# Every second gate and up pair of three feed-forward blocks by seven block products in place of eight

## The chip, the cores and the metric

The kernel runs on one core of a Trainium2 chip. The metric is device microseconds of one execution; lower is better. The inputs are float32, and the result is compared with a float32 reference.

## The reference

512 tokens of width 1024 go through a first block (a mixer, then a squared-ReLU feed-forward of width 4096, then a norm) and through two layers of a second block. Each of these layers has a gated feed-forward, a mixer (attention with pooling in layer 0, a short convolution in layer 1) and a second gated feed-forward, each with a modulated norm ahead of it:

```python
def swiglu(h, wg, wu, wd):
    return (jax.nn.silu(h @ wg) * (h @ wu)) @ wd
...
    for l in range(DEPTH_2):
        mod = (c_act @ w_ada[l] + b_ada[l]).reshape(b, N_MOD, 1, D_MODEL)
        sh1, sc1, g1, sh2, sc2, g2, sh3, sc3, g3 = [mod[:, i] for i in range(N_MOD)]
        h = modulated_norm(x, norm_g[l, 0], sh1, sc1)
        x = x + 0.5 * g1 * swiglu(h, ffn_wg[l, 0], ffn_wu[l, 0], ffn_wd[l, 0])
        ...
        h = modulated_norm(x, norm_g[l, 2], sh3, sc3)
        x = x + 0.5 * g3 * swiglu(h, ffn_wg[l, 1], ffn_wu[l, 1], ffn_wd[l, 1])
```

`h` is 512 x 1024, `wg` and `wu` are 1024 x 2816, `wd` is 2816 x 1024.

## The kernel before

Activations lie transposed: a tile has 128 features as partitions and the 512 tokens as columns, so `h` is eight tiles. Each value is kept as two float32r parts, a rounded one and the remainder (`h[:, 0]`, `h[:, 1]`). A weight block is treated likewise: ACT casts it to `whi`, DVE subtracts to get `wlo`. One product is then three matmuls per 128 features: high by high, high by low, low by high (`mm3`, L146 to L148):

```python
        nc.tensor.matmul(o, lhsT=hi[:, k, :], rhs=x[:, 0, t0:t0 + tn], start=first, stop=False)
        nc.tensor.matmul(o, lhsT=hi[:, k, :], rhs=x[:, 1, t0:t0 + tn], start=False, stop=False)
        nc.tensor.matmul(o, lhsT=lo[:, k, :], rhs=x[:, 0, t0:t0 + tn], start=False, stop=last)
```

A gated block (`ffn_glu`, `ffn`) has 22 pairs: pair m holds 128 columns of the gate weights and 128 of the up weights, 1 MB in one load. `wload` (L123) brings it into one of two staging tiles; `wblock` casts (L135) and subtracts (L136) the two units into two of four `whi` and two of four `wlo` buffers; `gemm` makes 24 matmuls for the gate and 24 for the up product, each group into one of five PSUM banks (`acc`). `evac` applies Silu to the gate (ACT, L768), multiplies by the up product (DVE, L770), and `split` writes the two parts of `y` (ACT L211, DVE L212). After 8, 7 and 7 pairs, `down` multiplies the `y` so far by its part of `wd` and adds the result to the residual (L306). All y, h and some attention tiles share a pool of 20 slots (`act`).

The last `down` of a block is tied to the next norm: `sumsq` gathers squares, and `norm_parts` computes, for each half of the tokens, the scale (`sums`) and the tiles (`tiles`: L276 makes the scaled `ht` in one of two buffers, L283 adds the shift and rounds, L284 makes the low part). `lead` then runs the first two pairs of the next block on the first 256 tokens, while the second half of the norm is still being made, and after it on the second 256.

The modulation (`ada_setup`) is 72 steps, each a 1 MB load into one buffer and two multiply-and-sum instructions on DVE (L790). `wblock` starts one step each time it is called (`ada_step`), except in the attention, where they are held back. The first block's feed-forward, the first gated block and the stage after the attention carry them.

Nothing in the text fixes the order on an engine, except where it asks for it: the program is traced, and a scheduler issues each engine's instructions by priority (place in the text) and readiness in its own model of the chip. Between `order_pe` and `free_pe` PE keeps the order of the text; before the change that is from the last two products of a `down` with a norm to the end of `lead`. Each engine works through its instructions in the order written, and a load waits on SP's queue for its buffer.

Of the kernel before, what the change touches and what calls it, by code (L numbers as in the profile page):

```python
# [17 lines left out]
T = 512  # L18
# [8 lines left out]
class Net:  # L27
    def __init__(self, ctx, tc, a, out):
        self.ctx, self.tc, self.nc, self.a, self.out = ctx, tc, tc.nc, a, out
        pool = lambda name, bufs, **kw: ctx.enter_context(tc.tile_pool(name=name, bufs=bufs, **kw))  # L30
        self.const = pool("const", 1)
        self.act = pool("act", 20)
        self.xv = pool("xv", 4)
        self.stg = pool("stg", 2)
        self.whl = pool("whl", 4)
        self.work = pool("work", 2)
        self.acc_p = pool("acc", 5, space=PSUM)
        self.ms_p = pool("ms", 3, space=PSUM)
        self.ada_todo = []
        self.ada_hold = False  # L40
        self.tail, self.late = [], []
        self.setup()

# [210 lines left out]

    def norm_parts(self, hs, half, gcols, shcols, pre=None):
        nc = self.nc
# [13 lines left out]
        def tiles():  # L270
# [3 lines left out]
            for k in range(8):  # L274
                t = self.wk("ht", (128, 256), 2)
                nc.vector.scalar_tensor_tensor(out=t, in0=self.xs(k, t0, 256), scalar=gcols[:, k:k + 1],  # L276
# [20 lines left out]
    def down(self, src, kn, xs, gcol, nxt=None, opened=()):  # L297
# [48 lines left out]
        if pre is not None:  # L346
            g = self.wk("fg", (128, 8), 1)
            nc.vector.tensor_tensor(out=g, in0=nxt["g"], in1=pre, op=ALU.mult)
        parts = [self.norm_parts(hs, half, g, nxt.get("sh"), pre) for half in range(2)]
        self.order_pe()  # L350
# [22 lines left out]
    def lead(self, wus, hs, done):  # L373
        for c, (part, t0) in enumerate((((0, 1, 2), 0), ((3,), 0), ((0, 1), 256), ((2, 3), 256))):
# [6 lines left out]
            for ps, j in zip(pss, part):  # L381
                done(j, ps, t0)

    def mixer1(self):
# [321 lines left out]

    def ffn(self, hs, groups, upblk, evac, dnsrc, gcol, nxt):
        m0 = 0
        for gi, gn in enumerate(groups):
# [22 lines left out]
            while len(ys) < gn:  # L732
                ws, outs = upblk(m0 + len(ys))
                n = len(ws) // outs
                for o in range(outs):
                    d = self.slot("y")
                    pss = [self.gemm([w], hs)[0] for w in ws[n * o:n * o + n]]
                    evac(d, pss, 0, 512)
                    ys.append(d)
            last = gi == len(groups) - 1  # L740
            r = self.down(dnsrc(gi), gn, ys, gcol, nxt if last else None)
            m0 += gn
# [17 lines left out]
    def ffn_glu(self, hs, l, i, gcol, nxt):  # L760
# [11 lines left out]

        return self.ffn(hs, FF2_GROUPS, up, evac, lambda gi: a[f"w_dn_{l}{i}{gi}"], gcol, nxt)

    def ada_setup(self):
        nc, a = self.nc, self.a
        c = self.ada_p = self.ctx.enter_context(self.tc.tile_pool(name="ada", bufs=1))
        self.SS2 = c.tile([128, 512], F32, name="SS2")
        cb = c.tile([128, 1024], F32, name="cb")
        nc.gpsimd.dma_start(out=cb, in_=a["c_rep"])  # L780
        nc.scalar.activation(out=cb, in_=cb, func=AF.Silu)
        self.mod = [c.tile([128, 72], F32, name=f"mod{l}") for l in range(2)]
        self.dmod = [c.tile([128, 48], F32, name=f"dmod{l}") for l in range(2)]

# [24 lines left out]
    def nspec(self, l, n):  # L809
        return {"g": self.dmod[l][:, 16 * n:16 * n + 8], "sh": self.mod[l][:, 24 * n:24 * n + 8]}  # L810

    def gate(self, l, n):
# [313 lines left out]
    def run(self):  # L1126
# [5 lines left out]
        for l in range(2):  # L1132
            hs = self.ffn_glu(hs, l, 0, self.gate(l, 0), self.nspec(l, 1))
            hs = (self.attn if l == 0 else self.conv)(hs, self.nspec(l, 2), self.gate(l, 1))
            hs = self.ffn_glu(hs, l, 1, self.gate(l, 2), self.nspec(1, 0) if l == 0 else "out")

# [111 lines left out]
```

## Time and profile before

| | us |
|---|---|
| median of three runs (2736.5 to 2742.88) | 2737.88 |
| the profiled execution | 2739.53 |
| its span, first to last instruction | 2737.4 |
| PE busy in it | 2696.5 |
| DVE busy | 1425.5 |
| ACT busy | 856.5 |

The granted clock was 0.997 over the span. The page gives busy time by engine, the groups of instructions by line and the loads. Queries of the trace give waits by engine (who waited, for whom, how long), single instructions in order of time, and busy time in chosen stretches. A matmul's duration is modelled; the distance between the starts of neighbours is not.

### The profile page before, as it was taken

To read this page: it belongs to the slowest core of one execution; us is meant where nothing else is said; L and a number is where in the kernel's file an instruction comes from. 1 tells how busy PE (TensorE), PEld (TensorE's weight loads), DVE (VectorE), ACT (ScalarE), POOL (GpSimd) and SP (SyncE) were. 2 spreads that over 40 slices of the span, in tenths; PEclk is the share of its full clock that TensorE was granted. 3 is DMA by queue.
4 is the path that set the end of the run, shared out by engine and by line. 5 is a ranking of instruction groups with operands and counts; after the bars stand their busy time and mean duration, and the time that the engine had idled before them with its cause. 6 is when DMAs were issued, how large, how long until landed. Compare 5 with 4: busy or idle time off the path is not lost.

```text
span 2737.4 us, 32001 instructions
## 1 busy us (share of the span) xinstructions
PE 2696.5 (99%) x13188; PEld 2273.0 (83%) x13188; DVE 1425.5 (52%) x2282; ACT 856.5 (31%) x1288; POOL 69.0 (3%) x98
## 2 busy tenths in 40 slices
PE   8999999999999999999999999999999999999999
PEld 6888888788888888888878888888888888888888
DVE  6556733476656855557676333353333454533333
ACT  5322222333223322224553222232222332332221
POOL 0000000000000000001210000000000000000000
PEclk9999999999999999999999999999999999999999
DMA  4211133355455455553223232323222223233232
GB/s 170 75 65 51 40 129 104 125 189 185 185 202 197 147 197 210 197 180 134 80 104 127 93 102 91 102 76 108 93 99 96 97 81 104 79 106 101 91 106 72
DMA packets 51281, 327.96 MB, mean 120 GB/s; under 512 B 5776, under 2 KB 6416, under 8 KB 17088
## 3 DMA queue, kind: packets, MB, share of 16 engines
q1 hardware_dynamic: 50400, 323.37, 33.8%
q0 software_dynamic: 736, 2.56, 0.3%
q8 instruction: 103, 1.69, 0.2%
q14 instruction: 42, 0.34, 0.0%
HBM read 323.81 MB, written 2.10 MB: 119 GB/s over the span
## 4 chain that ended last, share of the span: by engine, by line
PE 90%; DVE 5%; DMA 2%; issue 1%; ACT 1%; POOL 1%; SPq 0%; DVEq 0%; POOLq 0%; ACTq 0%
PE acc L147 27%; PE acc L146 27%; PE acc L148 27%; PE ms L590 2%; DMA ada<-in_w_ada 1%; DVE wlo L136 1%; PE acc L179 1%; PE acc L180 1%; PE acc L178 1%; DVE ada L790 1%; PE ms L628 1%; PE acc L206 1%; PE acc L205 1%; PE acc L204 0%; PE ms L568 0%
## 5 line engine op out<-in xcount | busy, mean ns | idle before, releaser
L135 ACT CAST whi<-w 128x1024 fp32r<-128x1024 f32 (+1 forms) x468 | 482.1, 1030 | 1537.7 <-PE acc L147 1434.0
L146 PE MATMUL acc<-h,whi 128*128 128x512 f32 (+1 forms) x2352 | 891.6, 379 | 9.0 <-ACT h L283 5.4
L147 PE MATMUL acc<-h,whi 128*128 128x512 f32 (+1 forms) x2352 | 885.7, 377 | 8.6 <-DVE h L284 5.1
L148 PE MATMUL acc<-h,wlo 128*128 128x512 f32 (+1 forms) x2352 | 883.5, 376 | 0.0
L136 DVE TENSOR_TENSOR wlo<-w,whi 128x1024 fp32r<-128x1024 f32 (+1 forms) x468 | 559.9, 1197 | 460.4 <-ACT whi L135 449.0
L147 PEld LDWEIGHTS acc<-h,whi 128*128 128x128 f32 x2352 | 445.3, 189 | 89.1 <-DVE h L284 6.8
L146 PEld LDWEIGHTS acc<-h,whi 128*128 128x128 f32 x2352 | 445.1, 189 | 88.8 <-ACT h L283 6.6
L148 PEld LDWEIGHTS acc<-h,wlo 128*128 128x128 f32 x2352 | 445.1, 189 | 77.5
L146 PE MATMUL acc<-y,whi 128*128 128x512 f32 (+1 forms) x1112 | 415.5, 374 | 0.0
L147 PE MATMUL acc<-y,whi 128*128 128x512 f32 (+1 forms) x1112 | 414.6, 373 | 0.0
L148 PE MATMUL acc<-y,wlo 128*128 128x512 f32 (+1 forms) x1112 | 414.4, 373 | 0.0
L147 PEld LDWEIGHTS acc<-y,whi 128*128 128x128 f32 x1112 | 209.5, 188 | 37.6 <-DVE y L212 0.9
L146 PEld LDWEIGHTS acc<-y,whi 128*128 128x128 f32 x1112 | 209.6, 188 | 36.8
L148 PEld LDWEIGHTS acc<-y,wlo 128*128 128x128 f32 x1112 | 209.5, 188 | 36.3
L790 DVE SCALAR_TENSOR_TENSOR ada<-ada,cb 128x1024 f32<-128x1024 f32 x144 | 174.8, 1222 | 105.9 <-DMA ada<-in_w_ada 105.8
L306 DVE SCALAR_TENSOR_TENSOR xt<-acc,dmod,xt 128x512 f32<-128x512 f32 (+1 forms) x124 | 86.6, 698 | 250.9 <-PE acc L148 250.7
L770 DVE TENSOR_TENSOR e<-acc,e 128x512 f32<-128x512 f32 (+1 forms) x92 | 60.3, 656 | 228.1 <-PE acc L148 227.8
L211 ACT CAST y<-e 128x512 fp32r<-128x512 f32 (+1 forms) x140 | 81.5, 583 | 56.4 <-DVE e L755 37.1
L212 DVE TENSOR_TENSOR y<-e,y 128x512 fp32r<-128x512 f32 (+1 forms) x140 | 89.4, 640 | 9.0 <-ACT y L211 8.9
L590 PEld LDWEIGHTS ms<-kq 128*128 128x128 f32 x448 | 56.3, 192 | 3.1
L283 ACT ACTIVATE h<-ht,mod 128x256 fp32r<-128x256 f32 x96 | 44.0, 502 | 45.6 <-DVE ht L276 45.6
L304 DVE TENSOR_TENSOR xt<-xt,acc 128x512 f32<-128x512 f32 (+1 forms) x44 | 28.0, 637 | 55.6 <-PE acc L148 55.6
(268 smaller groups left out, 2089.4 us busy)
## 6 DMA issues: line engine op xcount, KB each, us to landing
w<-in_w_gu SPq DMA_DIRECT2D x88, 1024.0 KB, 4.9
ada<-in_w_ada SPq DMA_DIRECT2D x72, 1024.0 KB, 6.4
w<-in_w_ff SPq DMA_DIRECT2D x32, 1024.0 KB, 4.8
w<-in_w_dn SPq DMA_DIRECT2D x32, 896.0 KB, 4.5
w<-in_w_dn SPq DMA_DIRECT2D x16, 1024.0 KB, 4.8
w<-in_w_fq SPq DMA_DIRECT2D x8, 1024.0 KB, 4.8
w<-in_w_gg SPq DMA_DIRECT2D x8, 1024.0 KB, 6.1
w<-in_w_cx SPq DMA_DIRECT2D x8, 1024.0 KB, 4.8
```

The costliest lines, as they stand in the source:

```text
L135: nc.scalar.copy(hi[:, :n], w[:, o:o + n])
L136: nc.vector.tensor_tensor(out=lo[:, :n], in0=w[:, o:o + n], in1=hi[:, :n].bitcast(F32), op=ALU.subtract)
L146: nc.tensor.matmul(o, lhsT=hi[:, k, :], rhs=x[:, 0, t0:t0 + tn], start=first, stop=False)
L147: nc.tensor.matmul(o, lhsT=hi[:, k, :], rhs=x[:, 1, t0:t0 + tn], start=False, stop=False)
L148: nc.tensor.matmul(o, lhsT=lo[:, k, :], rhs=x[:, 0, t0:t0 + tn], start=False, stop=last)
L211: nc.scalar.copy(h, src)
L212: nc.vector.tensor_tensor(out=dst[:, 1, t0:t0 + tn], in0=src, in1=h.bitcast(F32), op=ALU.subtract)
L283: nc.scalar.activation(out=h, in_=t, func=AF.Identity, bias=shcols[:, k:k + 1])
L306: nc.vector.scalar_tensor_tensor(out=x, in0=ps[:, :tn], scalar=gcol[:, m:m + 1], in1=x, op0=ALU.mult, op1=ALU.add)
L590: nc.tensor.matmul(ps[:, c * 64:(c + 1) * 64].rearrange("p (n b) -> p n b", b=b), lhsT=K[:, s], rhs=half(Q[:, s], 1), start=True, stop=True)
L770: nc.vector.tensor_tensor(out=y, in0=pss[1][:, :tn], in1=t, op=ALU.mult)
L790: nc.vector.scalar_tensor_tensor(out=w[:, i, :], in0=w[:, i, :], scalar=1.0, in1=cb, op0=ALU.mult, op1=ALU.mult, accum_out=self.mod[l][:, ...
```

## The change

In the last three gated blocks (layer 0's second, layer 1's first and second) the pairs 3, 5, ... 21 are computed by a seven-product scheme for 2 x 2 blocks: the weights of a pair are cut into gate and up by two halves of the 1024 features, the tokens into two halves of 256. `seven` makes four sums of weight blocks (three in a tile `S`, one in place in the staging tile), seven casts, their low parts in four subtractions, seven products of four feature tiles and 256 tokens each, and puts gate and up together again in `U`. `token_sums` makes the four sums of token blocks once per block, after pair 2, from the scaled norm tiles, which are kept in four slots (`keep`) in place of the two `ht` buffers. PE's order is that of the text from pair 3 up to the block's last `down`. The modulation's results move to another pool, so that its pool can be closed after the attention and its space be used for the sums; `ffn` starts two more modulation steps ahead of each `down` of the squared-ReLU block.

```diff
-    def norm_parts(self, hs, half, gcols, shcols, pre=None):
+    def norm_parts(self, hs, half, gcols, shcols, pre=None, keep=None):
...
-                t = self.wk("ht", (128, 256), 2)
+                t = self.wk("ht", (128, 256), 2) if keep is None else keep[k // 2][:, k % 2, t0:t0 + 256]
...
+        keep = None
+        if "sums" in nxt:
+            keep = self.B = [self.act.tile([128, 2, 512], F32, tag="slot", name="hb") for _ in range(4)]
+            self.sh = nxt["sh"]
...
+    def hilo(self, dst, src):
+        nc = self.nc
+        nc.scalar.copy(dst[:, 0], src)
+        nc.vector.tensor_tensor(out=dst[:, 1], in0=src, in1=dst[:, 0].bitcast(F32), op=ALU.subtract)
+
+    def token_sums(self, hs):
+        nc = self.nc
+        B, sh = self.B, self.sh
+        self.B = None
+        pairs = lambda t: t.rearrange("p a (k n) -> p a k n", k=2)
+        ds = self.wk("dsh", (128, 4), 1)
+        nc.vector.tensor_tensor(out=ds, in0=sh[:, 4:8], in1=sh[:, 0:4], op=ALU.subtract)
+        T = [[], [], [], []]
+        for j in range(2):
+            b1, b2 = B[j], B[2 + j]
+            b11, b12, b21, b22 = b1[:, :, 0:256], b1[:, :, 256:512], b2[:, :, 0:256], b2[:, :, 256:512]
+            for i in range(4):
+                T[i].append(pairs(self.slot("T") if i == 2 else self.slot("T", self.sx)))
+            nc.vector.tensor_tensor(out=b11, in0=b12, in1=b11, op=ALU.subtract)
+            self.hilo(T[0][j], b11)
+            for i in range(2):
+                k = 2 * j + i
+                nc.vector.scalar_tensor_tensor(out=b12[:, i], in0=b22[:, i], scalar=ds[:, k:k + 1], in1=b12[:, i],
+                                               op0=ALU.add, op1=ALU.subtract)
+            self.hilo(T[2][j], b12)
+            for i in range(2):
+                nc.vector.scalar_tensor_tensor(out=b22[:, i], in0=b22[:, i], scalar=sh[:, 4 + 2 * j + i:5 + 2 * j + i],
+                                               in1=b11[:, i], op0=ALU.add, op1=ALU.subtract)
+            self.hilo(T[1][j], b22)
+            for i in range(2):
+                nc.vector.scalar_tensor_tensor(out=b21[:, i], in0=b21[:, i], scalar=sh[:, 4 + 2 * j + i:5 + 2 * j + i],
+                                               in1=b22[:, i], op0=ALU.add, op1=ALU.subtract)
+            self.hilo(T[3][j], b21)
+        tok = lambda t: [(t[k // 2][:, 0, k % 2], t[k // 2][:, 1, k % 2]) for k in range(4)]
+        blk = lambda k0, n0: [(hs[k0 + k][:, 0, n0:n0 + 256], hs[k0 + k][:, 1, n0:n0 + 256]) for k in range(4)]
+        self.rhs = {1: blk(0, 0), 2: blk(4, 0), 3: blk(4, 256), 4: tok(T[3]), 5: tok(T[0]), 6: tok(T[1]), 7: tok(T[2])}
+
+    def seven(self, src, d):
+        nc = self.nc
+        w = self.wload(src)
+        S = self.sx.tile([128, 1536], F32, tag="S", name="S", bufs=1)
+        A = [w[:, 512 * i:512 * i + 512] for i in range(4)]
+        S1, S2, S4 = (S[:, 512 * i:512 * i + 512] for i in range(3))
+        op = {}
+
+        def parts(src, ps):
+            n = 512 * len(ps)
+            hi = self.whl.tile([128, 1024], F32R, tag="whi", name="whi")
+            lo = self.whl.tile([128, 1024], F32R, tag="wlo", name="wlo")
+            for i, p in enumerate(ps):
+                c = slice(512 * i, 512 * i + 512)
+                nc.scalar.copy(hi[:, c], src[:, c])
+                op[p] = tuple(t[:, c].rearrange("p (k m) -> p k m", m=128) for t in (hi, lo))
+            nc.vector.tensor_tensor(out=lo[:, :n], in0=src, in1=hi[:, :n].bitcast(F32), op=ALU.subtract)
+
+        def comb(out, a, b, how):
+            nc.vector.tensor_tensor(out=out, in0=a, in1=b, op=how)
+
+        parts(w[:, 0:1024], (1, 2))
+        comb(S1, A[2], A[3], ALU.add)
+        comb(S2, S1, A[0], ALU.subtract)
+        parts(S[:, 0:1024], (5, 6))
+        comb(A[2], A[0], A[2], ALU.subtract)
+        comb(S4, A[1], S2, ALU.subtract)
+        parts(w[:, 1024:2048], (7, 4))
+        parts(S4, (3,))
+        self.ada_step()
+
+        def prod(p):
+            ps = self.acc()[:, 0:256]
+            hi, lo = op[p]
+            for k in range(4):
+                xh, xl = self.rhs[p][k]
+                nc.tensor.matmul(ps, lhsT=hi[:, k, :], rhs=xh, start=(k == 0), stop=False)
+                nc.tensor.matmul(ps, lhsT=hi[:, k, :], rhs=xl, start=False, stop=False)
+                nc.tensor.matmul(ps, lhsT=lo[:, k, :], rhs=xh, start=False, stop=(k == 3))
+            return ps
+
+        U = self.sx.tile([128, 4, 256], F32, tag="U", name="U", bufs=1)
+        p1, u2, u3, v = (U[:, i] for i in range(4))
+        e = self.wk("e1", bufs=3)
+        y = self.wk("e2")
+        nc.scalar.copy(p1, prod(1))
+        comb(u2, prod(6), p1, ALU.add)
+        comb(e[:, 0:256], prod(2), p1, ALU.add)
+        comb(u3, prod(7), u2, ALU.add)
+        ps = prod(5)
+        comb(u2, ps, u2, ALU.add)
+        comb(v, ps, u3, ALU.add)
+        comb(e[:, 256:512], prod(3), u2, ALU.add)
+        nc.scalar.activation(out=e, in_=e, func=AF.Silu)
+        comb(y[:, 256:512], v, e[:, 256:512], ALU.mult)
+        comb(v, prod(4), u3, ALU.add)
+        comb(y[:, 0:256], v, e[:, 0:256], ALU.mult)
+        self.split(d, y)
...
             while len(ys) < gn:
-                ws, outs = upblk(m0 + len(ys))
+                m = m0 + len(ys)
+                if seven is not None and m >= 3 and m % 2:
+                    if m == 3:
+                        self.order_pe()
+                    d = self.slot("y")
+                    self.seven(seven(m), d)
+                    ys.append(d)
+                    continue
+                ws, outs = upblk(m)
...
+                if seven is not None and m == 2:
+                    self.token_sums(hs)
             last = gi == len(groups) - 1
+            if last and seven is not None:
+                self.free_pe()
+            for _ in range(2 if gcol is None else 0):
+                self.ada_step()
             r = self.down(dnsrc(gi), gn, ys, gcol, nxt if last else None)
...
-        c = self.ada_p = self.ctx.enter_context(self.tc.tile_pool(name="ada", bufs=1))
+        self.ada_es = ExitStack()
+        c = self.ada_p = self.ada_es.enter_context(self.tc.tile_pool(name="ada", bufs=1))
...
-            hs = (self.attn if l == 0 else self.conv)(hs, self.nspec(l, 2), self.gate(l, 1))
-            hs = self.ffn_glu(hs, l, 1, self.gate(l, 2), self.nspec(1, 0) if l == 0 else "out")
+            if l:
+                xs.close()
+            hs = (self.attn if l == 0 else self.conv)(hs, self.sums_spec(l, 2), self.gate(l, 1))
+            if l == 0:
+                self.ada_es.close()
+                xs = ExitStack()
+                self.sx = xs.enter_context(self.tc.tile_pool(name="sums", bufs=6))
+            else:
+                self.sx = self.ctx.enter_context(self.tc.tile_pool(name="sums2", bufs=6))
+            hs = self.ffn_glu(hs, l, 1, self.gate(l, 2), self.sums_spec(1, 0) if l == 0 else "out")
```

## Rows read from the trace of the kernel before

**Rows 1.** Page, part 1: busy us (share of the span) xinstructions, by engine.
```profile
PE 2696.5 (99%) x13188; PEld 2273.0 (83%) x13188; DVE 1425.5 (52%) x2282; ACT 856.5 (31%) x1288; POOL 69.0 (3%) x98
```

**Rows 2.** Waits of PE, whole span: waiter, what released it, total, times, longest.
```profile
PE acc L146 <- ACT h L283: 5.4, 5, 2.0
PE acc L147 <- DVE h L284: 5.1, 6, 1.3
...
PE ms L105 <- DVE mod L802: 0.8, 1, 0.8
```

**Rows 3.** Timeline of PE: first and last of 110, then of 50 matmuls.
```profile
2382.92 0.28 PE L147 MATMUL acc<-h,whi 128*128 128x256 f32 x1
...
2396.00 0.28 PE L148 MATMUL acc<-h,wlo 128*128 128x256 f32 x1
...
2396.82 0.40 PE L146 MATMUL acc<-h,whi 128*128 128x512 f32 x1
...
2407.93 0.39 PE L147 MATMUL acc<-h,whi 128*128 128x512 f32 x1
```

**Rows 4.** Groups of DVE by form: busy us, mean ns | idle before, releaser.
```profile
L136 DVE TENSOR_TENSOR wlo<-w,whi 128x1024 fp32r<-128x1024 f32 x396 | 484.5, 1225 | 411.9 <-ACT whi L135 402.0 <-PE ms L431 3.0
...
L212 DVE TENSOR_TENSOR y<-e,y 128x512 fp32r<-128x512 f32 x116 | 79.5, 686 | 8.9 <-ACT y L211 8.9
...
L770 DVE TENSOR_TENSOR e<-acc,e 128x512 f32<-128x512 f32 x80 | 55.3, 691 | 228.0 <-PE acc L148 227.8 <-issue 0.2
L284 DVE SCALAR_TENSOR_TENSOR h<-ht,mod,h 128x256 fp32r<-128x256 f32 x96 | 42.8, 480 | 2.1 <-ACT h L283 1.9
...
L212 DVE TENSOR_TENSOR y<-e,y 128x256 fp32r<-128x256 f32 x24 | 9.9, 420 | 0.1
```

**Rows 5.** Groups of ACT by form, same columns.
```profile
L135 ACT CAST whi<-w 128x1024 fp32r<-128x1024 f32 x396 | 416.6, 1052 | 1296.4 <-PE acc L147 1192.8 <-issue 59.9 <-PE acc L180 29.4
L211 ACT CAST y<-e 128x512 fp32r<-128x512 f32 x116 | 72.0, 621 | 53.6 <-DVE e L755 36.9 <-DVE e L770 16.4
...
L768 ACT ACTIVATE e<-acc 128x512 f32<-128x512 f32 x80 | 47.0, 588 | 0.0
...
L768 ACT ACTIVATE e<-acc 128x256 f32<-128x256 f32 x16 | 6.1, 381 | 11.7 <-PE acc L148 11.7
```

**Rows 6.** Timeline of DVE: start, us, instruction, idle before it.
```profile
2402.68 1.23 DVE L136 TENSOR_TENSOR wlo<-w,whi 128x1024 fp32r<-128x1024 f32 x1 [2.69 <-ACT whi L135]
2407.30 0.69 DVE L770 TENSOR_TENSOR e<-acc,e 128x512 f32<-128x512 f32 x1 [3.39 <-PE acc L148]
2408.14 1.23 DVE L136 TENSOR_TENSOR wlo<-w,whi 128x1024 fp32r<-128x1024 f32 x1 [0.15 <-ACT whi L135]
2409.28 0.68 DVE L212 TENSOR_TENSOR y<-e,y 128x512 fp32r<-128x512 f32 x1
```

**Rows 7.** Page, part 6: loads, KB each, us from issue to landing.
```profile
w<-in_w_gu SPq DMA_DIRECT2D x88, 1024.0 KB, 4.9
ada<-in_w_ada SPq DMA_DIRECT2D x72, 1024.0 KB, 6.4
```

**Rows 8.** Windows: last norm's end to pair 3, last gated block.
```profile
core 0: us, PE busy (x) PEld busy (x) DVE busy (x) ACT busy (x) POOL busy (x), PEclk, DMA share, GB/s
...
2388.60:2407.40 18.80, 18.80 (x115) 16.88 (x114) 7.42 (x11) 7.24 (x11) 0.00 (x0) 1.00 0.34 112
```

**Rows 9.** Windows: first feed-forward block; norm ahead of the first gated block.
```profile
547.00:875.00 328.00, 324.92 (x1496) 272.35 (x1497) 212.30 (x318) 106.56 (x151) 2.36 (x3) 0.99 0.52 191
...
900.00:905.00 5.00, 2.96 (x24) 2.55 (x22) 4.48 (x13) 3.63 (x8) 0.70 (x1) 1.00 0.27 111
905.00:910.00 5.00, 3.70 (x18) 3.51 (x19) 5.00 (x12) 1.20 (x3) 0.00 (x0) 0.70 0.54 187
```

**Rows 10.** Line L790's instructions: duration ns min/median/max.
```profile
L790 DVE SCALAR_TENSOR_TENSOR ada<-ada,cb x144: 1208/1221/1228, 548.5 to 1466.5; 128x1024 f32<-128x1024 f32 x144
```

**Rows 11.** Page, part 5: weight loads of one line, mean ns of one.
```profile
L147 PEld LDWEIGHTS acc<-h,whi 128*128 128x128 f32 x2352 | 445.3, 189 | 89.1 <-DVE h L284 6.8
```

More of the change, by code (lines that the diff above doesn't have):

```diff
@@ L41, in __init__ @@
         self.tail, self.late = [], []
+        self.B = self.sh = None
         self.setup()
@@ L348, in down @@
             nc.vector.tensor_tensor(out=g, in0=nxt["g"], in1=pre, op=ALU.mult)
-        parts = [self.norm_parts(hs, half, g, nxt.get("sh"), pre) for half in range(2)]
+        keep = None
+        if "sums" in nxt:
+            keep = self.B = [self.act.tile([128, 2, 512], F32, tag="slot", name="hb") for _ in range(4)]
+            self.sh = nxt["sh"]
+        parts = [self.norm_parts(hs, half, g, nxt.get("sh"), pre, keep) for half in range(2)]
         self.order_pe()
@@ L705, in gmlp, with ffn @@
         return gm
-    def ffn(self, hs, groups, upblk, evac, dnsrc, gcol, nxt):
+    def ffn(self, hs, groups, upblk, evac, dnsrc, gcol, nxt, seven=None):
         m0 = 0
@@ L771, in evac @@
             self.split(d, y, t0, tn)
-        return self.ffn(hs, FF2_GROUPS, up, evac, lambda gi: a[f"w_dn_{l}{i}{gi}"], gcol, nxt)
+        return self.ffn(hs, FF2_GROUPS, up, evac, lambda gi: a[f"w_dn_{l}{i}{gi}"], gcol, nxt,
+                        None if self.B is None else lambda m: a[f"w_gu_{l}{i}"][m])
     def ada_setup(self):
         nc, a = self.nc, self.a
-        c = self.ada_p = self.ctx.enter_context(self.tc.tile_pool(name="ada", bufs=1))
+        self.ada_es = ExitStack()
+        c = self.ada_p = self.ada_es.enter_context(self.tc.tile_pool(name="ada", bufs=1))
         self.SS2 = c.tile([128, 512], F32, name="SS2")
@@ L781, in ada_setup @@
         nc.scalar.activation(out=cb, in_=cb, func=AF.Silu)
-        self.mod = [c.tile([128, 72], F32, name=f"mod{l}") for l in range(2)]
-        self.dmod = [c.tile([128, 48], F32, name=f"dmod{l}") for l in range(2)]
+        self.mod = [self.const.tile([128, 72], F32, name=f"mod{l}") for l in range(2)]
+        self.dmod = [self.const.tile([128, 48], F32, name=f"dmod{l}") for l in range(2)]
         def one(l, j):
@@ L810, in nspec, with sums_spec @@
         return {"g": self.dmod[l][:, 16 * n:16 * n + 8], "sh": self.mod[l][:, 24 * n:24 * n + 8]}
+    def sums_spec(self, l, n):
+        return {"sums": True, **self.nspec(l, n)}
     def gate(self, l, n):
```

## The prediction

> **What bounds the kernel now.** I read the page's busy times first: the matmul engine PE is busy for 99% of the span, the vector engine DVE for 52%, ACT for 31% [rows 1]. A busy PE alone doesn't prove a bound, because the ends of matmuls are modelled, so the second view is who PE waited for. The reader should see there that apart from one at the kernel's start the largest stand at the norms in front of the blocks (ACT h, DVE h), that the whole list of 18 rows adds up to 37 us, and that the gate and up products wait for nothing once a norm is over [rows 2]. The third view, single matmuls in order of time, shows PE at a fixed rhythm: 50 matmuls of 512 columns from the first to the last row take 11.11 us, 0.2267 us each; 110 matmuls of 256 columns take 13.08 us, 0.1200 us each [rows 3]. Halving the columns doesn't quite halve the time: some 13 ns per matmul stay. In mid-block, then, time is matmul count times rhythm, and what other engines do costs nothing while they keep ahead.
>
> **The products.** A gate and up pair is 48 matmuls of 512 columns: 48 x 0.2267 = 10.88 us. With seven block products it is 7 x 4 x 3 = 84 matmuls of 256 columns: 84 x 0.1200 = 10.08 us. So 12.5% fewer columns are worth only 0.80 us, 7%. Pairs 3, 5, ... 21 of three blocks make 30: **-24.1 us**. The 256-column rhythm was read in a norm's lead, where three of the units alternate; a product here has one accumulator for 12 matmuls, as the 512-column pairs have, so I take the rhythm unchanged.
>
> Here a rule of the Trainium skill speaks against the change. "TensorE: Matmul & The Clock Gate", section "Back-to-back issue gap", says that in a stream of weight load and matmul pairs the spacing is set by both, and gives 81 ns at 128 columns and 131 ns at 512; a straight line between them, an estimate, has 98 ns at 256, by which 84 x 98 ns = 8.2 us would replace 48 x 131 ns = 6.3 us, and 30 pairs would lose 57 us. The rows here differ from it at 512 columns (0.2267 us), and at 256 the measured 0.1200 us contains one load per matmul; by the rows the sum stays a gain.
>
> **Work on DVE and ACT per changed pair.** Removed on DVE: two subtractions of 1024 columns, one product, one split, 2 x 1.225 + 0.691 + 0.686 = 3.83 us [rows 4]. Added: four sums of weight blocks at 0.686, low parts of seven operands (3 x 1.225 + 0.686), nine combinations of 256 columns at 0.42 and the split at 0.686: 2.74 + 4.36 + 3.78 + 0.69 = 11.57 us. ACT goes from 2 x 1.052 + 0.588 + 0.621 = 3.31 to seven casts at 0.621, a copy at 0.381, Silu and split: 5.94 us [rows 5]. Changed and unchanged pairs alternate, so against PE's 10.08 + 10.88 = 20.96 us stand 15.4 us of DVE (73%) and 9.3 of ACT (44%). Both fit, so I cost them at **0**. The cover is how early operands are ready. Four buffers hold the casts; a changed pair takes all four. The first two are free while the pair before runs; the third waits for that pair's gate (middle of its 10.88 us) and feeds the products p7 and p4, the first of which starts 4.3 us into the changed pair; the fourth waits for its up and feeds p3, 7.2 us in. The next pair's gate buffer is free after p1, p6, p2, 4.3 us in: cast 1.05 and low part 1.225 leave it ready at about 6.7 of 10.08 us, 3.4 us ahead. If the cover is gone, each us of lateness is a us per pair. DVE issues in the order that the scheduler wrote: it now sits idle before a low part or a product for 2.7 to 3.4 us while later work stands behind it [rows 6]. This order is what I cannot see. Bounds per changed pair: 0 (rhythm as now) and 2.1 us (the tail after p4, two combinations at 0.42 and a low part at 1.225, all ahead of the next gate). I take 0, since at 73% the order leaves DVE more than 5 us of room per two pairs.
>
> PSUM: products use five banks, one per 1.44 us, so a combination may be 4 us late before PE stops. Ends of groups: after pairs 7 and 21 the down product needs the last y at its 19th or 22nd matmul, 4.1 to 4.8 us in; p4's tail (0.42 + 0.42 + 0.621 + 0.686 = 2.15 us) is ahead of that: 0. The weight load into staging moves a little later with the third buffer; it lands in 4.9 us [rows 7], and two pairs take 20.96: 0.
>
> **Token sums, once per block.** For each of two pairs of row tiles: five subtractions of 512 columns, four of them low parts (5 x 0.686), and six of 256 with a column of scalars (6 x 0.480): 6.31 us, so with one tiny subtraction ahead 12.8 us of DVE and 8 x 0.621 = 5.0 us of ACT. They need both halves of the norm and must be done before the second product of pair 3. Between the norm's last low part and pair 3 lie 18.8 us, in which DVE is busy for 7.42 [rows 8]; of that, three low parts of pairs 3 and 4 (3.68 us) become other work or move, so 15.1 us are free, and 16.5 until p6. Wanted by then: the sums 12.8, two weight sums 1.37, two low parts 2.45, and pair 2's product and split 1.38: 18.0 us. DVE is 1.5 us short, and the chain sum, cast, low part adds some 0.5. I take **+2.0 us per block, +6.0 in all**. Bounds: 0, and 7 us per block (half of the free time lost to waits for ACT): 0 to +21. A gap on PE has an after-effect here: in the norm ahead of the first gated block PE idled 2.0 and 1.3 us of two slices of 5 us, and the granted clock read 0.70 in the second, a mixture of 2.4 and 1.2 GHz [rows 9]. Whether a stall of 2 us brings that I can't read; I charge nothing, and it belongs to the upper bound.
>
> **The kept norm tiles** go into four separate buffers instead of two that alternate. Same instructions; PE's waits for h with a shift add up to 10.5 us over the six norms that have one, three of them changed here [rows 2]: 0, bounds -3 and +1.
>
> **The modulation steps.** Eight of 72 (a 1 MB load that lands in 6.4 us [rows 7] and 2 x 1.221 = 2.4 us of DVE [rows 10], 8.8 in turn) move up, two ahead of each down of the first feed-forward block, past the loads of that down's weights on SP's queue. They share one buffer, so two more in a row can hold the next weight load on SP by 17.6 us, of which the pair already cast covers 10.88: 6.7 us, were one of the four places exposed in full. DVE in that block rises from 212 to 232 us of 328 [rows 9], behind PE still. They leave the attention's end, where one delays the norm by 0.8 [rows 2]. I take **0**, bounds -3 and +8.
>
> **Sum.** The profiled execution took 2739.5 us (span 2737.4); -24.1 + 6.0 gives 2721.4. It lay 1.65 above the median of 2737.88, so by the median **2720 us**; own range 2712 (nothing lost) to 2729 (15 us lost).
>
> **Rivals.** (1) *Half given back*: DVE's order makes the products wait now and then, 0.3 to 0.7 us per changed pair, 9 to 21 us: 2729 to 2741, about 2733. For it: DVE goes from 35% to 73% of PE's time and waits in order [rows 6]. Against: five banks and 3.4 us of lead. (2) *Slower, next pair's weights late*: the next gate's low part stands on DVE behind the whole tail of a changed pair, and PE idles 2.1 us at each of 30 changes: 63 us, 2783. The gain is gone at (24.1 - 6.0) / 30 = 0.6 us per pair; over 0.3%, 8.2 us, slower from 0.9. For it: priorities follow the program's text, in which the tail comes first. Against: today a low part of the next pair already runs between a product and its split [rows 6], so the order goes by readiness. (3) *Weight loads bind*: 84 loads of 0.189 us [rows 11], if 256 columns hid none of one behind another, make 15.9 us a pair, 5.0 more than now, 150 in 30: 2894 with the rest. The 0.1200 us speaks against; it decides from 0.130 us (10.88 / 84). The rule of the Trainium skill named above ("TensorE: Matmul & The Clock Gate") is this one in kind.
>
> **Chances.** Forecast 0.70, rival 1 0.16, rival 2 0.12, rival 3 0.02. What a measurement of this kernel can tell from no change is about 0.3%, 8.2 us: faster is below 2729.7, slower above 2746.1. The forecast is all faster; rival 1 is nearly all within; rivals 2 and 3 are slower: 0.71, 0.15, 0.14. The range reaches from 2712 to 2741, through rival 1; about 0.14 lies above and 0.05 below.
>
> **What would show it.** Right: 2520 more matmuls of 256 columns and 1440 fewer of 512, the former 0.12 us apart within and across the seven products; DVE busy near 1425 + 30 x 7.74 + 38 = 1695 us; PE waits of 1 to 3 us at the second product of pair 3 of each block and nowhere else in it; modulation steps ended before the attention. Wrong: PE waiting for the casts or low parts of the pair behind a changed one (rivals 1 and 2), a rhythm of 0.13 or more (rival 3), or a stall above 5 us at pair 3.

## The result, and the profile after

| | before | after |
|---|---|---|
| median, us (4 runs each) | 2740.38 | 2713.40 |
| profiled execution | 2739.53 | 2713.47 |
| its span | 2737.4 | 2711.7 |

The ratio is 0.9899, with a 95% interval of 0.9887 to 0.9912: 1% faster, 27.7 us by the ratio and 26.1 us between the profiled executions. The three medians of the kernel before in the later measurements lie between 2740.2 and 2741.8. The prediction said 2720 in a range of 2712 to 2741, with 0.71 on faster by more than 0.3%; the time lies in the range, 1.4 us above its low end.

The page's first part, after (answers to [rows 1]):

```profile
PE 2672.5 (99%) x14268; PEld 2302.2 (85%) x14268; DVE 1663.7 (61%) x2771; ACT 943.0 (35%) x1492; POOL 68.7 (3%) x98
```

PE lost 24.0 us of busy time, DVE gained 238 and ACT 87. DVE had been forecast at 1695; 1664 is less, and that will matter. The waits of PE, whole span (answers to [rows 2]; the same columns):

```profile
PE acc L147 <- ACT h L284: 5.4, 5, 2.1
PE acc L148 <- DVE h L285: 3.7, 5, 1.3
...
PE acc L148 <- DVE y L213: 1.3, 3, 0.9
```

Line numbers have moved: L146 to L148 of before are L147 to L149 now, and L462 to L464 are the matmuls of `seven`. The norms' waits are as before (5.4) or shorter (3.7 after 5.1). New is a wait of 1.3 us in three pieces for the last `y` of a group, in `down` (and 0.2 for its other part). No row names a product of a changed pair (L462 to L464): the waits that the forecast put at pair 3 do not exist.

Single matmuls, the edges of one changed pair in layer 0's second gated block (answers to [rows 3]):

```profile
1513.25 0.39 PE L149 MATMUL acc<-h,wlo 128*128 128x512 f32 x1
1513.48 0.28 PE L462 MATMUL acc<-h,whi 128*128 128x256 f32 x1
...
1523.49 0.40 PE L147 MATMUL acc<-h,whi 128*128 128x512 f32 x1
```

The pair begins at 1513.48 and the next one, unchanged, at 1523.49: 84 matmuls in 10.01 us, 0.1192 each. Each of the 30 changed pairs takes 10.01 us. Against the 10.88 of an unchanged one before, that is 26.1 us in 30. An unchanged pair between two changed ones now takes 10.91 (1523.49 to the next changed pair at 1534.40), which takes back about 0.8 us in all.

The time from one norm's first broadcast matmul (L105, after L106) to the next one's splits the span into stages, read from the timelines:

```
stage, us                            before    after   difference
up to the first of these norms        537.0    535.5     -1.5
squared-ReLU feed-forward             365.3    367.5     +2.2
layer 0, first gated block            368.9    370.0     +1.1
attention                             185.0    181.7     -3.3
layer 0, second gated block           365.9    355.9    -10.0
layer 1, first gated block            365.7    358.7     -7.0
convolution                           180.9    182.3     +1.4
layer 1, second gated block           368.8    360.0     -8.8
```

The three changed blocks give back 25.8 us, nearly the whole of the difference. The small ones among the others are partly scatter: in the eleven traces of this study the stage ahead of the first norm lies between 535.5 and 539.0. That the three blocks differ by 3 us among themselves, with the same ten changed pairs in each, is not explained here.

### The profile page after: what moved, and what is told of

Its sections match the earlier page's. It is cut to its first block, busy times and chain, and to the rows that moved or that the text cites. A ratio compares the mean times of both kernels' runs of the same rounds, so it can differ in the third digit from the quotient of the medians.

```text
span 2711.7 us, 35057 instructions
## 1 busy us (share of the span) xinstructions
PE 2672.5 (99%) x14268; PEld 2302.2 (85%) x14268; DVE 1663.7 (61%) x2771; ACT 943.0 (35%) x1492; POOL 68.7 (3%) x98
## 4 chain that ended last, share of the span: by engine, by line
PE 89%; DVE 5%; DMA 3%; ACT 1%; issue 1%; POOL 0%; SPq 0%; DVEq 0%; POOLq 0%; ACTq 0%
PE acc L148 23%; PE acc L147 23%; PE acc L149 23%; PE acc L462 4%; PE acc L464 4%; PE acc L463 4%; DMA ada<-in_w_ada 2%; PE ms L691 2%; DVE ada L907 1%; DVE wlo L137 1%; PE acc L180 1%; PE acc L181 1%; PE acc L179 1%; PE ms L729 1%; PE acc L207 1%
## 5 line engine op out<-in xcount | busy, mean ns | idle before, releaser
L136 ACT CAST whi<-w 128x1024 fp32r<-128x1024 f32 (+2 forms) x408 | 418.4, 1026 | 1121.9 <-PE acc L148 872.5
L147 PE MATMUL acc<-h,whi 128*128 128x512 f32 (+1 forms) x1872 | 705.3, 377 | 8.9 <-ACT h L284 5.4
L148 PE MATMUL acc<-h,whi 128*128 128x512 f32 (+1 forms) x1872 | 699.5, 374 | 7.0 <-DVE h L285 3.7
L149 PE MATMUL acc<-h,wlo 128*128 128x512 f32 (+1 forms) x1872 | 697.3, 373 | 0.0
L137 DVE TENSOR_TENSOR wlo<-w,whi 128x1024 fp32r<-128x1024 f32 (+2 forms) x408 | 485.4, 1191 | 236.9 <-ACT whi L136 230.0
L148 PE MATMUL acc<-y,whi 128*128 128x512 f32 (+1 forms) x1112 | 414.8, 373 | 1.4 <-DVE y L213 1.3
L147 PE MATMUL acc<-y,whi 128*128 128x512 f32 (+1 forms) x1112 | 415.2, 373 | 0.2 <-ACT y L212 0.2
L147 PEld LDWEIGHTS acc<-h,whi 128*128 128x128 f32 x1872 | 356.0, 190 | 69.6 <-ACT h L284 6.6
L149 PE MATMUL acc<-y,wlo 128*128 128x512 f32 (+1 forms) x1112 | 414.0, 372 | 0.0
L148 PEld LDWEIGHTS acc<-h,whi 128*128 128x128 f32 x1872 | 356.1, 190 | 68.0 <-DVE h L285 4.9
L149 PEld LDWEIGHTS acc<-h,wlo 128*128 128x128 f32 x1872 | 356.2, 190 | 59.4
L148 PEld LDWEIGHTS acc<-y,whi 128*128 128x128 f32 x1112 | 209.4, 188 | 40.1 <-DVE y L213 3.8
L147 PEld LDWEIGHTS acc<-y,whi 128*128 128x128 f32 x1112 | 209.4, 188 | 37.5 <-ACT y L212 0.6
L149 PEld LDWEIGHTS acc<-y,wlo 128*128 128x128 f32 x1112 | 209.4, 188 | 36.3
L462 PE MATMUL acc<-T,whi 128*128 128x256 f32 x480 | 135.5, 282 | 0.0
L464 PE MATMUL acc<-T,wlo 128*128 128x256 f32 x480 | 135.5, 282 | 0.0
L463 PE MATMUL acc<-T,whi 128*128 128x256 f32 x480 | 135.2, 282 | 0.0
L442 DVE TENSOR_TENSOR wlo<-w,whi 128x1024 fp32r<-128x1024 f32 x60 | 73.3, 1222 | 64.2 <-ACT whi L440 64.2
```

The source lines that it names most:

```text
L136: nc.scalar.copy(hi[:, :n], w[:, o:o + n])
L137: nc.vector.tensor_tensor(out=lo[:, :n], in0=w[:, o:o + n], in1=hi[:, :n].bitcast(F32), op=ALU.subtract)
L462: nc.tensor.matmul(ps, lhsT=hi[:, k, :], rhs=xh, start=(k == 0), stop=False)
L463: nc.tensor.matmul(ps, lhsT=hi[:, k, :], rhs=xl, start=False, stop=False)
L464: nc.tensor.matmul(ps, lhsT=lo[:, k, :], rhs=xh, start=False, stop=(k == 3))
```

## The experiments

The ratio of each run is to the kernel before, measured beside it; the changed kernel is 0.9899 in this measure. Differences in us between two runs are differences of their medians.

### Without the token sums

```diff
                 if seven is not None and m == 2:
-                    self.token_sums(hs)
+                    blk = lambda k0, n0: [(hs[k0 + k][:, 0, n0:n0 + 256], hs[k0 + k][:, 1, n0:n0 + 256]) for k in range(4)]
+                    self.rhs = {p: blk(4 * (p % 2), 256 * (p // 2 % 2)) for p in range(1, 8)}
+                    self.B = None
```

> The token sums are left out; the products that take them read unsummed parts of h. Theory (the sums are wholly hidden beside PE): no change from the changed kernel, 2713 +-3 us, each changed pair still 10.01 us on PE. Rival (they do cost the 2 us per block of my sum, and something else gave it back): 2707 us, three stretches near pair 3 shorter by 2 us each.

Measured: 2713.67 us, ratio 0.9902 (0.9887 to 0.9917), no difference from the changed kernel. One thing besides the sums differs: a changed pair takes 10.07 us here, not the 10.01 that were expected, although all 84 matmuls follow each other without a wait:

```profile
1511.18 0.28 PE L462 MATMUL acc<-h,whi 128*128 128x256 f32 x1
...
1521.25 0.40 PE L147 MATMUL acc<-h,whi 128*128 128x512 f32 x1
```

That is 2.0 us in 30 pairs, and the three blocks are 1.7 us longer than with the sums (1076.3 for 1074.6 us). So the comparison is not clean by itself, but with this taken off the token sums still cost nothing that can be measured. They are not small: the windows (us, then busy us and count of PE, PEld, DVE, ACT, POOL, granted clock, DMA share, GB/s) show them. Of the changed kernel, the first row is two pairs in mid-block, the second the stretch of the last block from the norm's second half to the start of pair 3:

```profile
1514.00:1535.00 21.00, 21.00 (x135) 19.10 (x135) 14.29 (x23) 8.84 (x15) 0.00 (x0) 1.00 0.30 107
2369.00:2390.00 21.00, 21.00 (x134) 19.11 (x134) 20.50 (x39) 12.37 (x23) 0.00 (x0) 1.00 0.15 51
```

The same stretch of the kernel without the sums:

```profile
2369.00:2390.00 21.00, 21.00 (x135) 19.11 (x134) 12.04 (x19) 8.83 (x17) 0.00 (x0) 1.00 0.28 100
```

DVE is busy for 20.5 of 21 us with them and for 12.0 without, and PE for 21.00 in both. The work fits, but barely. The mid-block row has the steady load: 14.3 of 21 us, where 15.4 had been counted.

Why it fits is seen in DVE's order of time, changed kernel, at pair 3 of the last block, which starts at 2389.46 (start, duration, instruction):

```profile
2387.14 0.69 DVE L445 TENSOR_TENSOR w<-w 128x512 f32<-128x512 f32 x1
2387.74 0.68 DVE L445 TENSOR_TENSOR S<-w,S 128x512 f32<-128x512 f32 x1
2388.34 1.22 DVE L442 TENSOR_TENSOR wlo<-S,whi 128x1024 fp32r<-128x1024 f32 x1
2389.48 1.22 DVE L442 TENSOR_TENSOR wlo<-w,whi 128x1024 fp32r<-128x1024 f32 x1
2390.61 0.69 DVE L885 TENSOR_TENSOR e<-acc,e 128x512 f32<-128x512 f32 x1
2391.21 0.68 DVE L442 TENSOR_TENSOR wlo<-S,whi 128x512 fp32r<-128x512 f32 x1
2392.02 0.69 DVE L213 TENSOR_TENSOR y<-e,y 128x512 fp32r<-128x512 f32 x1
2392.63 1.29 DVE L392 TENSOR_TENSOR T<-hb,T 128x512 fp32r<-128x512 f32 x2
```

Two things are to be seen. First, most instructions start about 80 ns before the one ahead of them has ended: a sum of 512 columns lasts 0.69 us, but the next starts 0.60 after it; one of 1024 lasts 1.22 and takes 1.14. Adding durations counts these 80 ns once too often for each instruction. "Perfetto Trace Analysis" of the Trainium skill, section "Optimizing Scalar/DVE Operations", has a reason: the profiled time of an instruction contains the acknowledgement of its write, and that part overlaps with the next instruction. The trace agrees that they overlap, by 80 ns here; that it is the acknowledgement which overlaps, no row shows. Second, the low parts of the last token sums (T, 2392.63) stand behind pair 2's split and three low parts of weights: what the product p6 does not need was put behind what it needs. The low part that p6 waits for (S, 2388.34) ends at 2389.56, 1.3 us before p6 begins.

### The low parts of the token sums made twice

```diff
         nc.scalar.copy(dst[:, 0], src)
         nc.vector.tensor_tensor(out=dst[:, 1], in0=src, in1=dst[:, 0].bitcast(F32), op=ALU.subtract)
+        nc.vector.tensor_tensor(out=dst[:, 1], in0=src, in1=dst[:, 0].bitcast(F32), op=ALU.subtract)
```

> Each of the eight low parts of the token sums is made twice: 8 x 0.69 = 5.5 us more of DVE per block, before pair 3. Theory (DVE is full there, 20.5 of 21 us, and only what p6 needs decides): p6 starts late, PE waits 2 to 5.5 us per block, 2719 to 2730 us. Rival (the sums needed late can be put off, so room is left): 2713 +-3 us and no wait.

Measured: 2727.69 us, ratio 0.9954 (0.9938 to 0.9969), 14 us more than the changed kernel. The first changed pair of the three blocks takes 16.6, 11.9 and 16.9 us, the other 27 take 10.01. So the stretch was full: 5.5 us of added work made these pairs 6.6, 1.9 and 6.8 us longer. Windows around pair 3 of the three blocks (columns as above):

```profile
1470.00:1500.00 30.00, 25.36 (x168) 23.09 (x166) 29.52 (x57) 14.59 (x29) 0.00 (x0) 1.00 0.10 36
1836.00:1866.00 30.00, 28.37 (x194) 26.27 (x193) 29.48 (x55) 15.01 (x28) 0.00 (x0) 1.00 0.20 70
2374.00:2404.00 30.00, 25.55 (x167) 23.19 (x166) 29.53 (x57) 15.39 (x29) 0.00 (x0) 0.95 0.10 36
```

DVE is busy for 29.5 of 30 us in each; PE was idle for 4.6, 1.6 and 4.5. In the first of these blocks DVE's order shows what PE waits for:

```profile
1496.26 1.28 DVE L392 TENSOR_TENSOR T<-hb,T 128x512 fp32r<-128x512 f32 x2
1497.46 1.28 DVE L393 TENSOR_TENSOR T<-hb,T 128x512 fp32r<-128x512 f32 x2
1498.67 1.21 DVE L443 TENSOR_TENSOR wlo<-S,whi 128x1024 fp32r<-128x1024 f32 x1
```

The low part of the sums of weights that p6 waits for (S, 1498.67) now stands behind four low parts of T, two of them the repeats; p6's third matmul, the first to need it, starts at 1499.93. Two of the pairs grew by more than the added work, but no idle time is longer than it: the rest is TensorE's clock. Windows just after the gaps of the first and third block, and two neighbouring matmuls of the first:

```profile
1498.00:1503.00 5.00, 3.07 (x14) 3.07 (x15) 4.71 (x8) 0.62 (x1) 0.00 (x0) 0.68 0.24 34
2402.00:2407.00 5.00, 3.19 (x15) 3.19 (x16) 4.53 (x7) 0.62 (x1) 0.00 (x0) 0.50 0.10 20
```

```profile
1501.16 0.41 PE L464 MATMUL acc<-T,whi 128*128 128x256 f32 x1
1501.38 0.41 PE L465 MATMUL acc<-T,wlo 128*128 128x256 f32 x1
```

The granted clock reads 0.68 (partly 1.2 GHz) and 0.50 (1.2 GHz throughout), and matmuls start 0.21 us apart in place of 0.12. That makes the remaining 6.6 - 4.6 = 2.0 and 6.8 - 4.5 = 2.3 us. In the second block PE idled for 1.6 us and the granted clock stayed at 1.00. This is the after-effect of a gap that the prediction charged with nothing and left to its upper bound; the changed kernel has no gap there, and its granted clock reads 1.00 (window 2369 to 2390 above). The total lies in the range expected, 2719 to 2730 us; by block, the 2 to 5.5 us were missed on both sides. That the order in which the token sums are put off differs from block to block may be why the second block lost less; it was not tried.

### DVE in the order of the text

```diff
                     if m == 3:
-                        self.order_pe()
+                        self.order_pe(mybir.EngineType.DVE)
...
-    def order_pe(self):
-        self.region = self.tc.manual_schedule(engines={mybir.EngineType.PE})
+    def order_pe(self, *more):
+        self.region = self.tc.manual_schedule(engines={mybir.EngineType.PE, *more})
```

> DVE, too, keeps the order of the text from pair 3 to the last down of the three blocks; the same instructions. Theory (the order by readiness is what hides 11.6 us of DVE per changed pair): a changed pair's first products wait for the sums of weights and the next pair's gate for the tail, about 8 us per two pairs, and the downs wait too: 2900 to 3000 us; at the least the 2.1 us per changed pair of my rival, 2776. Rival (buffers give room enough whatever the order): under 2730 us.

Measured: 3116.17 us, ratio 1.1371 (1.1352 to 1.1390). The same instructions, 403 us more than the changed kernel, and 116 above the range expected. DVE around one changed pair of the first of the three blocks, which begins at 1704.5 (start, duration, instruction, idle before it):

```profile
1704.74 0.69 DVE L885 TENSOR_TENSOR e<-acc,e 128x512 f32<-128x512 f32 x1 [11.34 <-PE acc L149]
1706.12 0.69 DVE L213 TENSOR_TENSOR y<-e,y 128x512 fp32r<-128x512 f32 x1 [0.68 <-ACT y L212]
1706.72 1.22 DVE L442 TENSOR_TENSOR wlo<-w,whi 128x1024 fp32r<-128x1024 f32 x1
...
1724.45 0.69 DVE L213 TENSOR_TENSOR y<-e,y 128x512 fp32r<-128x512 f32 x1 [0.68 <-ACT y L212]
1725.06 2.35 DVE L137 TENSOR_TENSOR wlo<-w,whi 128x1024 fp32r<-128x1024 f32 x2
1738.76 0.69 DVE L885 TENSOR_TENSOR e<-acc,e 128x512 f32<-128x512 f32 x1 [11.35 <-PE acc L149]
```

DVE waits 11.3 us for the unchanged pair's products and only then starts on the operands of the changed one, whose PE time becomes 17.7 us (16.2 to 18.1 in 27 of 30 pairs); the low parts for the pair behind it follow the split of the changed pair. The waits of PE name both places:

```profile
PE acc L149 <- DVE wlo L137: 129.9, 51, 3.7
PE acc L464 <- DVE wlo L442: 92.9, 54, 3.1
```

The second row is inside the changed pairs, 92.9 us; the first, 129.9 us, is the casts' low parts of unchanged pairs and of the downs. PE pays for the gaps twice: the granted clock falls with them. The page's first part, and two windows:

```profile
PE 2838.2 (91%) x14268; PEld 2419.0 (78%) x14268; DVE 1667.9 (54%) x2771; ACT 944.7 (30%) x1492; POOL 69.4 (2%) x98
```

```profile
1700.00:1800.00 100.00, 82.00 (x397) 68.96 (x396) 38.92 (x54) 22.39 (x32) 0.00 (x0) 0.91 0.19 69
2800.00:2900.00 100.00, 79.36 (x386) 69.91 (x387) 43.74 (x66) 28.22 (x43) 0.00 (x0) 0.80 0.18 61
```

With PE busy for 82 and 79 of 100 us it stood at 0.91 and 0.80, a mixture of 2.4 and 1.2 GHz, where the changed kernel has 1.00. Of the 397 us between the profiled executions 166 are a longer busy time of PE for the same 14268 matmuls (2838.2 for 2672.5), and 232 are idle. This is rival 2 of the prediction, let loose: that the work fits by its size is not enough, the order in which DVE takes it has to hide it too.

### All pairs from 3 on

```diff
-                if seven is not None and m >= 3 and m % 2:
+                if seven is not None and m >= 3:
```

> All pairs from 3 to 21 by seven products, 19 per block in place of 10. DVE then has 11.57 us per pair against 10.01 of PE. Theory (DVE's sum per pair binds, and no work runs far ahead): 11.6 us or more per changed pair, +1.6 x 30 + 0.7 x 27 = 67 us: 2780 us. Rival (PE still binds): 27 x 0.87 = 23 us less, 2690 us.

Measured: 2696.77 us, ratio 0.9838 (0.9823 to 0.9852), faster than both kernels. My theory fell: by the sum of durations DVE would have bound at 11.6 us per pair, yet 51 of the 57 pairs take 10.0 us and the others 10.1 or 10.4. Windows over the five changed pairs of the first group and the seven of the second:

```profile
1495.00:1548.00 53.00, 52.80 (x431) 51.99 (x430) 51.71 (x90) 28.95 (x51) 0.00 (x0) 1.00 0.28 100
1591.00:1661.00 70.00, 70.00 (x588) 69.92 (x588) 66.88 (x119) 36.76 (x66) 0.00 (x0) 1.00 0.27 96
```

DVE is busy for 51.7 of 53 and 66.9 of 70 us: full or nearly so, with PE at its rhythm. By distances between starts a changed pair is 4 x 0.60 + 3 x 1.14 + 0.60 + 9 x 0.335 + 0.60 = 10.0 us, the same as PE's. 27 more changed pairs at 0.90 (10.91 to 10.01) would give 24.3 us; the blocks gave 20.9 (349.6, 351.1 and 353.0 us). The pairs of 10.1 and 10.4 took 1.7 us of the rest, and the downs wait 3.2 us for a last `y`, where they waited 1.5.

### All pairs, with 1.2 us more on DVE per pair

```diff
         parts(S4, (3,))
+        x = self.sx.tile([128, 512], F32, tag="X", name="X", bufs=1)
+        for _ in range(2):
+            comb(x, S2, S4, ALU.add)
         self.ada_step()
```

> All pairs from 3 on by seven products, each with two more sums of 512 columns on DVE whose result nobody reads: 1.2 us more. Theory (DVE stands at the edge, 9.6 of 10.0 us): it becomes the bound, each of 57 pairs takes 10.7 to 11.3 us, 2737 to 2770 us. Rival (there is room left in DVE's 83 ns overlaps): 2697 +-4 us.

Measured: 2732.22 us, ratio 0.9967 (0.9955 to 0.9979), 35 us more than all pairs without it and a little under the range expected. The mean pair takes 10.70 us, but no pair does: in each group of seven the first four take 10.0 and the other three 11.4 to 11.6. PE's wait is where it should be:

```profile
PE acc L467 <- DVE wlo L442: 22.2, 26, 0.9
```

and over one group of seven with the start of the down, windows:

```profile
1596.00:1676.00 80.00, 76.97 (x612) 74.50 (x611) 77.56 (x136) 38.27 (x68) 0.00 (x0) 1.00 0.29 99
```

In the last three pairs DVE is busy for 11.3 to 11.6 us of each, so it binds. A changed pair that needs 11.4 on DVE against 10.0 on PE uses up 1.4 us of DVE's lead, so the four pairs at 10.0 put the lead that DVE gains during a down at some 5 us (an estimate from these numbers, not read in a row). 11.4 less the added 2 x 0.60 is 10.2 us, the load of a pair on DVE, against 11.57 by durations. It would also explain all pairs above: such a lead covers an excess of 0.2 us for seven pairs.

### All pairs, the sums of weights on GpSimd

```diff
-        comb(S1, A[2], A[3], ALU.add)
-        comb(S2, S1, A[0], ALU.subtract)
+        gcomb(S1, A[2], A[3], ALU.add)
+        gcomb(S2, S1, A[0], ALU.subtract)
         parts(S[:, 0:1024], (5, 6))
-        comb(A[2], A[0], A[2], ALU.subtract)
-        comb(S4, A[1], S2, ALU.subtract)
+        gcomb(A[2], A[0], A[2], ALU.subtract)
+        gcomb(S4, A[1], S2, ALU.subtract)
```

Here `gcomb` is `nc.gpsimd.tensor_tensor` with the same operands; the all-pairs edit is kept.

> All pairs from 3 on by seven products, with the four sums of weight blocks on GpSimd in place of DVE. Theory (with all pairs PE binds at 10.0 us per pair, and DVE, full for 9.6 of 10.0, costs only the few pairs of 10.4): relieving DVE brings 0 to 3 us against the 2696.8 of all pairs. Rival (GpSimd is the slower engine, its copy of 512 columns took 0.99 us against DVE's 0.69, and its sums come late): the products p6 and p5 wait, over 2705 us.

Measured: 2709.17 us, ratio 0.9891 (0.9874 to 0.9907), 12 us more than all pairs on DVE. 48 pairs still take 10.0 us, but the first pairs of the blocks take 11.8 and the downs wait for the last `y` (6.8 us in two rows). Taking 2.4 us per pair off DVE made the kernel slower. POOL, mid-block:

```profile
1649.77 1.29 POOL L448 TENSOR_TENSOR S<-w 128x512 f32<-128x512 f32 x1 [3.66 <-DVE wlo L442]
...
1654.16 2.28 POOL L448 TENSOR_TENSOR S<-w,S 128x512 f32<-128x512 f32 x1
```

and DVE in the same time:

```profile
1650.06 1.28 DVE L445 TENSOR_TENSOR e<-U,e 128x256 f32<-128x256 f32 x1
...
1652.97 0.41 DVE L445 TENSOR_TENSOR U<-acc,U 128x256 f32<-128x256 f32 x1
...
1660.44 0.43 DVE L445 TENSOR_TENSOR e<-U,e 128x256 f32<-128x256 f32 x1
```

A sum of 512 columns takes 1.3 to 2.3 us on POOL; the four run without a pause from 1649.77 to 1656.44. While they run, DVE instructions whose operands all lie in SBUF are slow too: 256 columns take 1.28 us (1650.06) in place of 0.43 (1660.44, with POOL idle). A combination that takes one operand from PSUM (1652.97) keeps its 0.41. The groups by form (busy us, mean ns, idle before) show the same over the whole run, first for all pairs on DVE, then with the sums on POOL:

```profile
L445 DVE TENSOR_TENSOR e<-U,e 128x256 f32<-128x256 f32 x114 | 47.7, 418 | 1.4
L445 DVE TENSOR_TENSOR e<-acc,U 128x256 f32<-128x256 f32 x114 | 47.5, 417 | 2.8 <-PE acc L464 2.4
```

```profile
L445 DVE TENSOR_TENSOR e<-U,e 128x256 f32<-128x256 f32 x114 | 81.4, 714 | 1.6
L445 DVE TENSOR_TENSOR e<-acc,U 128x256 f32<-128x256 f32 x114 | 47.1, 413 | 5.6 <-PE acc L467 5.6
```

57 x 4 sums of 0.60 are 137 us taken off DVE, yet its busy time fell by 41 only, from 1829.8 to 1789.0 us. The waits of PE that grew are for this slower DVE, or for ACT behind it: for the last `y` 6.8 us where it was 3.2, for the norm's h from DVE (L285) 6.0 where it was 3.7, and for the low parts of the token sums 4.0 where it was nothing. In the first changed pair of the first block, while the POOL sums run (1501.90 to 1508.29):

```profile
1501.91 1.83 DVE L213 TENSOR_TENSOR y<-e,y 128x512 fp32r<-128x512 f32 x1
1503.67 3.48 DVE L392 TENSOR_TENSOR T<-hb,T 128x512 fp32r<-128x512 f32 x2
```

```profile
PE acc L466 <- DVE T L392: 4.0, 6, 0.7
```

The split takes 1.83 us in place of 0.69 and the two low parts of the token sums 3.48 in place of 1.28. The rival had the time right, but its cause is not seen: no row of PE's waits names POOL or the sums of weights. "SBUF — State Buffer" of the Trainium skill, section "Who interferes with whom", says of such pairs: a DVE instruction with two SBUF inputs contends with a GpSimd instruction that reads SBUF; one with at most one SBUF input, outside its 2-port modes, does not. The rows agree, with 0.85 us added to the instruction at 1650.06.

### The changed kernel, with 4.8 us more on DVE per changed pair

```diff
         parts(S4, (3,))
+        x = self.sx.tile([128, 512], F32, tag="X", name="X", bufs=1)
+        for _ in range(8):
+            comb(x, S2, S4, ALU.add)
         self.ada_step()
```

> The changed kernel, each changed pair with eight more sums of 512 columns on DVE whose result nobody reads: 4.8 us on 14.3 of 20.9 us per two pairs, 91%. Theory (only DVE's total per two pairs counts): still hidden, 2713 to 2718 us. Rival (DVE's order, in which added work stands ahead of products to be collected, costs long before the total is full): 0.5 us or more per changed pair, 2728 us or more.

Measured: 2717.81 us, ratio 0.9915 (0.9900 to 0.9930), 4 us more than the changed kernel, with intervals that overlap. All 30 changed pairs take 10.0 us. Two pairs in mid-block, window:

```profile
1626.10:1647.10 21.00, 21.00 (x134) 19.06 (x134) 19.00 (x30) 8.76 (x15) 0.00 (x0) 1.00 0.29 105
```

With unchanged pairs between the changed ones DVE may be 90% full and PE loses nothing, as expected if only the total over two pairs counts. What was lost lies beside the token sums, where DVE was full already: in the first and the third block the pair behind the first changed one waits 1.6 us for its low part and takes 1.9 us longer. The three blocks are 2.4 us longer in the profiled execution (357.8, 357.4 and 361.9 us).

### The modulation steps alone

```diff
             last = gi == len(groups) - 1
+            for _ in range(2 if gcol is None else 0):
+                self.ada_step()
```

This is the kernel before with this edit.

> The kernel before, with two more modulation steps ahead of each down of the squared-ReLU block and nothing else of the change. Theory (my term of 0): 2738 to 2742 us, up to 2 us more in the first feed-forward, up to 4 less around the attention. Rival (the loads hold back SP's weight loads): 2746 us or more.

Measured: 2738.88 us, ratio 0.9993 (0.9983 to 1.0002). No change that can be told. Two stages moved against each other, in the same directions as in the changed kernel: the first gated block takes 373.4 us, where it took 368.9, and the attention 180.3, where it took 185.0.

### PE without the fixed order

```diff
-                    if m == 3:
-                        self.order_pe()
...
-            if last and seven is not None:
-                self.free_pe()
```

> The changed kernel without the fixed order of PE from pair 3 to the block's last down; the scheduler places the products itself. Theory (readiness already gives nearly the order of the text, and PE is full): 2713 +-4 us. Rival (the scheduler pulls products of another pair or of the down between the seven, and the combinations on DVE and the banks then stop PE): 2725 us or more.

Measured: 2712.53 us, ratio 0.9893 (0.9875 to 0.9911). No difference: each changed pair still is 84 matmuls in a row, so with all its operands early PE gets the text's order anyway. The three blocks take 355.9, 358.7 and 360.0 us, the same as with it.

## Why the prediction was right

**The products.** The step held: PE is the bound in mid-block and 84 matmuls of 256 columns replace 48 of 512. The size was -24.1 and is -26.1 us: the lead's rhythm of 0.1200 was taken over, while in the seven products it is 0.1192 (10.01 us per pair). Why it is lower is open; one accumulator for 12 matmuls is not enough to explain it, since the kernel without token sums has that too, and 10.07 us per pair. The rule that spoke against the change, from "TensorE: Matmul & The Clock Gate" of the Trainium skill, does not describe this stream: by it the pair would have become longer, and it became 0.87 us shorter.

**DVE and ACT per changed pair at 0.** Right, and shown from both sides: 4.8 us more per changed pair cost 4 us in all, all of DVE in the order of the text cost 403 us. The sum itself, 11.57 us, was too large: 10.2 us by the steady rate with DVE as the bound, 10.0 by distances between starts. [Rows 6] already showed it: the low part at 2408.14 lasts 1.23, and the split behind it starts 1.14 later. I added means of single durations.

**Token sums, +6.0.** This term failed; they cost 0. The step that failed is "DVE is 1.5 us short": 18.0 us were wanted against 16.5. With some 80 ns less for each of about 29 instructions, 18.0 becomes 15.7, and the sums that only later products need were not wanted by p6 at all; how much each of the two gave was not separated. The lower bound, 0, was right, and the experiment with doubled low parts shows that the margin was small: the stretch has no 5.5 us to spare. The same experiment gives the price of a gap that the sum had left at nothing: 2.0 and 2.3 us behind idle times of 4.6 and 4.5, none behind 1.6. Here no gap came.

**Modulation steps, kept tiles, ends of groups at 0.** Right within scatter: the modulation alone is 0.9993. In the changed kernel its steps end at 1241 us, ahead of the attention (1273), PE's waits for h with a shift are 9.1 us where they were 10.5, and the downs wait 1.5 us in all for a last `y`.

**The sum.** -24.1 + 6.0 = -18.1 was forecast, and -26.1 + 0 was measured. That this equals the 26.1 between the profiled executions to the digit is chance: the three blocks give 25.8, the other stages near zero together. Both terms were off toward a longer time, by 2.0 and 6.0 us, so the errors added up, and the range held by 1.4 us only. Rivals 1 and 3 show no trace; rival 2 needs another order on DVE, and then costs more than the 63 us that were put on it, since the operands of the changed pair itself come late too and the clock falls.

## What to carry to other kernels

Where one engine is full, take a block product away from it even at three times the element-wise work, as long as the others' sum per stage, counted from start to start of their instructions, stays below it and their order keeps the full engine's operands early; here it paid up to the point where both stood at 10.0 us per pair. Count an engine's load from distances between starts in a dense stretch, not from durations. Before moving element-wise work to GpSimd, look at what DVE does at the same time from SBUF.

## What was not expected of the hardware

DVE instructions overlap by some 80 ns in the trace, which is 13% of a pair's load here (10.0 for 11.57 us). GpSimd's sums stretched a DVE product of two SBUF operands from 0.43 to 1.28 us and left those with a PSUM operand at 0.41. Behind idle times of 4.6 and 4.5 us of PE the granted clock read 0.68 and 0.50 in a stretch of 5 us, and matmuls of 256 columns started 0.21 us apart in place of 0.12. The rhythm of these matmuls was 0.1200 us in the lead, which alternates between accumulators, and 0.1192 in the seven products, which have one for 12 matmuls; without the token sums it was 0.1199, though each product had one accumulator there too. So the alternation does not explain the difference, and its cause is open.
